# Moving the g_pre product of five first-norm tiles from the vector engine to GpSimd, and the rstd into the scale of the fp16 split

## The chip, the cores and the metric

The kernel runs on one core of a Trainium2 chip. The metric is the device time of one execution in microseconds; the time of a kernel is the median of its runs. A profiled execution leaves a trace, whose span runs from the first to the last instruction on the core; its own time is a little longer than that span. The engines are named as in the trace: PE is TensorE's matrix multiply and PEld its weight load, DVE is VectorE, ACT is ScalarE, POOL is GpSimd and SP is SyncE, which here only issues DMAs.

## What is computed

One layer of a hybrid decoder trunk on a sequence of 1024 tokens, 1024 wide, in float32. What matters here is its beginning, the first norm and the projection that follows it:

```python
def rms_norm(x, g):
    var = jnp.mean(x * x, axis=-1, keepdims=True)
    return x * lax.rsqrt(var + RMS_EPS) * g

h = rms_norm(x, norm_mix_pre)                 # x: 1024 tokens x 1024
proj = h @ w_in                               # q, k, v, conv inputs, two gates
q, k, v, cb, cc, cx, g_att, g_conv = split(proj)
m = sigmoid(g_att) * (attention(q, k, v) @ w_att) + sigmoid(g_conv) * (conv(cb, cc, cx) @ w_conv)
x = x + rms_norm(m @ w_out, norm_mix_post)
# then a convolutional feed-forward of width 2816, with a norm of its own
```

The attention is stick-breaking and strictly causal, in 8 heads of 64.

## The kernel before

**Precision.** Products of matrices are made of fp16 pairs. A float32 operand is scaled by a power of two and split into a high half (the fp16 rounding) and a low half (the rest), and three passes of fp16 matmuls, high by high, high by low and low by high, stand for one float32 product. The scale of the normed activations is `s_h`, a power of two worked out from the largest gain.

**Tiles.** The tokens are eight tiles of 128 (tile 0 to 7), each a [128 tokens, 1024] float32 tile `x`, loaded by SP at the start. A tile is normed and then turned, so that the model dimension lies on the partitions, into `hT` (high and low half). Tiles 0 to 2 are turned by PE. Tiles 3 to 7 are split first and then turned by the DMA's transpose, and these five are the ones that the change touches.

**One of these five tiles, before.** `norm` (line 253): ACT squares the row and sums it (`sumsq`, line 66); DVE makes mean plus epsilon (line 256, a 128x1 instruction); GpSimd raises it to the power of -0.5 (line 257, 128x1), which gives rstd; DVE multiplies the tile in place by rstd, a scalar for each partition, and by `gb`, the gain broadcast to all partitions (line 259, 128x1024). `turn_dma` (line 302): ACT writes the high half, the tile times `s_h` rounded to fp16 (line 304, 128x1024); DVE writes the low half, the tile times `s_h` less the high half (line 305, 128x1024); SP issues a DMA transpose for each half (line 308).

**What surrounds them.** PE makes the value products `pv` (line 367) of tiles 0 to 3, then the q and the k of the first head pair for the first 512 tokens (line 459, `pq` and `pk`), then the values of tile 4, then attention scores `z` (line 595) between further projections ("fills"). ACT and DVE split the weights on their way: `wh_v` at lines 520 and 522, `wh_q` and `wh_k` at lines 445 and 446. They also take the high and low half of q and k out of the accumulator (lines 474 and 476), move the value tiles (lines 381 to 398), and finish the turned tile 2 (lines 526 and 527) and tile 0 (lines 543 and 544).

**Order.** Inside this part nothing is ordered by hand on any engine but PE. Each step is put into a plan with its engine, an assumed cost, what it reads and what it writes; a list scheduler then runs through all of them with those costs and writes out one order for each engine: "V" for DVE, "A" for ACT, "G" for GpSimd, "SP" for the queue of SP, and "PE". Each engine works through its instructions in that order. Most PE steps keep the order in which they are written; the scores, the weighted values and the sums of the weight scales are fitted in where the plan has them ready. A step's rank among those that are ready comes from how late it may be for what follows it, or from a due time that it is given (tiles 4, 5, 6 and 7 have 0, 3, 4 and 5 us). The tile of rstd (`r_pre`) comes from a ring of 8 small tiles.

Of the kernel before, what the change touches and what calls it, by code (L numbers as in the profile page):

```python
# [20 lines left out]
AF = mybir.ActivationFunctionType  # L21
ALU = mybir.AluOpType
# [20 lines left out]
TURNED = (0, 1, 2, 4, 5, 6)  # L43
KEPT = (3,)
ONE = 2.0 ** 14


class Layer:
# [84 lines left out]
    def mixer(self, mid):  # L133
        tc, nc, a = self.tc, self.nc, self.a
        hT = self.hp.tile([P, 2, KD, T], F16, tag="hT", name="hT")
        with ExitStack() as ph1:
# [6 lines left out]
            nc.gpsimd.memset(self.mask[:, :NH], 0.0)  # L143
            nc.gpsimd.memset(self.mask[:, NH:], ONE)
            nc.gpsimd.affine_select(self.mask[:, NH:], self.mask[:, NH:], [[1, P]], ALU.is_ge, 0.0, base=0,
# [5 lines left out]
            if True:  # L151
# [7 lines left out]
                gb = self.slot([P, D], F32, "g_pre")  # L159
                xt = {}  # L160
# [25 lines left out]
                with tc.manual_schedule(engines={ET.PE, ET.DVE, ET.Activation, ET.SP, ET.Pool}):  # L186
                    pl = Plan(dict(s=12, ws=4, wh=8, pm=3, z=2, o=1, sm=8, rb=8, sc=16, e=3, w=2, wt=1, cr=4, o16=4))
                    pl.landed = 0.9
                    pl.own, pl.loaded = {"PE": 0.0}, 22.0
                    vec, act, pe, pool = nc.vector, nc.scalar, nc.tensor, nc.gpsimd  # L190
                    NOTE = lambda: Buf(None, lambda: {})

                    def given(p, tile, avail=0.0):
                        b = Buf(p, None)
                        b.tile, b.avail = tile, avail
                        pl.caps[p] -= 1
                        return b

                    def V(cost, fn, r, w, **kw):
                        return pl.add("V", cost, fn, r, w, **kw)  # L200

                    def A(cost, fn, r, w, **kw):
                        return pl.add("A", cost, fn, r, w, **kw)

                    def M(cost, fn, r, w, seq=True):
                        return pl.add("PE", cost, fn, r, w, seq=seq)

                    def two_banks(name):
                        return pat.tile([P, KD, P], F32, tag="z", name=name, bufs=2)
# [7 lines left out]
                    gbb = given("s", gb, 14.4)  # L217
# [6 lines left out]
                    g_s, g_c, g_t = NOTE(), NOTE(), NOTE()  # L224
                    h0, h1 = slice(0, NH), slice(NH, D)
                    s_h, inv_h = gs[:, 3:4], gs[:, 4:5]
# [19 lines left out]
                    gpb = Buf("z", lambda: two_banks("g_ps"))  # L246
                    ps2 = Buf("pm", lambda: pm.tile([P, NH], F32, tag="pm", name="g2"))
                    for c in range(2):
                        M(0.94, lambda c=c: pe.matmul(gpb.t.rearrange("p k t -> p (k t)")[:, ds(c * NH, NH)], on1[0:1, :],
                                                      gr[0:1, ds(c * NH, NH)], start=True, stop=True), [one_row, g_row], [(gpb, str(c))])  # L250
                    M(0.3, lambda: pe.matmul(ps2.t[:, 0:2], self.ones[0:1, :], g_c.t["g16"][0:1], start=True, stop=True),
                      [g_c], [ps2])
                    def norm(tt):
                        r, x = Buf("sm", lambda: self.small(f"r_pre{tt}")), xs[tt]
                        A(1.25, lambda: self.sumsq(xt[tt], r.t[:, 0:1], f"n_pre{tt}"), [x], [r])
                        V(0.15, lambda: vec.tensor_scalar(r.t[:, 1:2], r.t[:, 0:1], 1.0 / D, EPS, ALU.mult, ALU.add), [], [r])
                        pl.add("G", 0.6, lambda: pool.tensor_tensor(r.t[:, 2:3], r.t[:, 1:2], self.neghalf, ALU.pow), [], [r])
                        g = gpb if tt < 2 else gbb
                        V(1.28, lambda: vec.scalar_tensor_tensor(
                            xt[tt], xt[tt], r.t[:, 2:3], g.t.rearrange("p k t -> p (k t)") if tt < 2 else gb,  # L260
                            ALU.mult, ALU.mult), [r, g], [x])

                    def norm_halves(tt, first=(), prior=(), then=None):
                        r, x = Buf("sm", lambda: self.small(f"r_pre{tt}")), xs[tt]
# [36 lines left out]

                    def turn_dma(tt, due=1e9):
                        b, x = Buf("s", lambda: self.slot([P, 2, D], F16, f"x16_{tt}")), xs[tt]
                        A(1.06, lambda: act.activation(b.t[:, 0, :], xt[tt], AF.Copy, scale=s_h), [x, g_s], [(b, "0")], due=due)
                        V(1.27, lambda: vec.scalar_tensor_tensor(b.t[:, 1, :], xt[tt], s_h, b.t[:, 0, :], ALU.mult, ALU.subtract),
                          [x, g_s, (b, "0")], [(b, "1")], due=due)
                        for e in range(2):
                            j = pl.add("SP", 1.27, lambda e=e: nc.sync.dma_start_transpose(hT[:, e, :, ds(tt * P, P)], b.t[:, e, :]),
                                       [(b, str(e))], [(hb[tt], str(e))], due=due + 5)
                            j.load = 1.0  # L310
# [210 lines left out]
                    for i in range(4):  # L521
                        V(1.25, lambda i=i: vec.scalar_tensor_tensor(wvb[i].t[:, 1, :], st[i], bv.t["s"], wvb[i].t[:, 0, :],
                                                                     ALU.mult, ALU.subtract), [raw_v[i], bv, (wvb[i], "0")], [(wvb[i], "1")])
                    norm(2)
                    turn_pe(2)
                    A(1.1, lambda: act.activation(hT[:, 0, :, ds(2 * P, P)], pt[2].t, AF.Copy, scale=s_h), [pt[2], g_s], [(hb[2], "0")])
# [9 lines left out]
                    for i in range(4):  # L536
                        v_pass(1, (2 * i, 2 * i + 1), ((0, 1),), last=i == 3)
                    v_end(0)
                    norm(3)
                    turn_dma(3)  # L540
                    v_pass(2, range(8), ((0, 1),), last=True)
                    v_end(1)
# [12 lines left out]
                    for tt, due in ((4, 0.0), (5, 3.0), (6, 4.0), (7, 5.0)):  # L555
                        norm(tt)
                        turn_dma(tt, due)
# [39 lines left out]
                    def unit(u):  # L597
# [23 lines left out]
                        for h in range(2):  # L621
                            def scan(h=h):
                                x = e.t[:, h, NH - w:][:, ::-1]
                                vec.tensor_tensor_scan(x, x, m[:, ::-1], ONE if diag else cr.t[:, h:h + 1], ALU.mult, ALU.max)  # L624
                            V(0.08 + 1.13 * r, scan, [] if diag else [cr], [(e, str(h))], due=PACE[1])
# [8 lines left out]
                        def turn(x):  # L634
                            pl.add("SP", 1.25, lambda: nc.sync.dma_start_transpose(
                                wt.t[:, x, :2 * w // P, ds(t * P, P)], w16.t[:, x, :2 * w]),
                                [(w16, str(x))], [(wt, f"{x}{t}")], due=PACE[4]).load = 1.5 * r
                        A(0.21 + 0.85 * r, lambda: act.activation(dst(0), src(), AF.Copy, bias=-ONE), [e], [(w16, "0"), turns[2]], due=PACE[2])  # L638
                        turn(0)

                        def low():
                            if not diag:
                                f = lambda x: w16.t[:, x, :2 * w].rearrange("p (h s) -> p h s", h=2)
                                vec.scalar_tensor_tensor(f(1), e.t[:, :, NH - w:], ONE, f(0), ALU.subtract, ALU.subtract)
                                return
                            for h in range(2):
                                vec.scalar_tensor_tensor(dst(1)[:, h], src()[:, h], ONE, dst(0)[:, h], ALU.subtract, ALU.subtract)
                        V(0.08 + 1.1 * r + 0.08 * diag, low, [e, (w16, "0")], [(w16, "1")], due=PACE[3])
# [32 lines left out]
                    k = 0  # L681
# [1324 lines left out]
```

## Time and profile before

| | us |
|---|---|
| median of 3 runs | 1250.1 |
| lowest and highest of the runs | 1249.38, 1251.72 |
| profiled execution, its own time | 1250.39 |
| span of the profiled execution | 1248.7 |
| PE busy in the span | 1233.2 |

In the views, a row of the timeline gives the start of an instruction in us from the span's start, its duration, the engine, the line, the operation with what it writes and reads, and in brackets how long its engine was idle before it and what ended that. A row of the windows gives a stretch and the busy time of each engine in it, with the number of instructions, then the clock granted to TensorE as a share of full speed, the busy share of the DMA engines and GB/s. A row of waits gives who waited for whom, the total in us, how often, and the longest.

### The profile page before, as it was taken

To read this page: it belongs to the slowest core of one execution; us is meant where nothing else is said; L and a number is where in the kernel's file an instruction comes from. 1 tells how busy PE (TensorE), PEld (TensorE's weight loads), DVE (VectorE), ACT (ScalarE), POOL (GpSimd) and SP (SyncE) were. 2 spreads that over 40 slices of the span, in tenths; PEclk is the share of its full clock that TensorE was granted. 3 is DMA by queue.
4 is the path that set the end of the run, shared out by engine and by line. 5 is a ranking of instruction groups with operands and counts; after the bars stand their busy time and mean duration, and the time that the engine had idled before them with its cause. 6 is when DMAs were issued, how large, how long until landed. Compare 5 with 4: busy or idle time off the path is not lost.

```text
span 1248.7 us, 16478 instructions
## 1 busy us (share of the span) xinstructions
PE 1233.2 (99%) x6065; PEld 559.4 (45%) x6065; DVE 1018.6 (82%) x1605; ACT 856.1 (69%) x1247; POOL 86.3 (7%) x113
## 2 busy tenths in 40 slices
PE   9999999999999999999989999999999999999997
PEld 4444444444444444444444444444444444444443
DVE  7888889856998675559899999699589879969866
ACT  7766666736758565755666679778778967878434
POOL 1100000000000000001100001001100300111003
PEclk9999999999999999999999999999999999999999
DMA  8755577660224111656953205415921961594607
GB/s 276 157 128 116 136 129 180 148 150 29 74 74 129 34 65 54 233 189 149 222 144 133 71 23 214 169 34 99 257 82 19 203 184 34 104 251 142 179 1 135
DMA packets 148931, 160.80 MB, mean 129 GB/s; under 512 B 114425, under 2 KB 114553, under 8 KB 148850
## 3 DMA queue, kind: packets, MB, share of 16 engines
q1 hardware_dynamic: 138480, 123.05, 35.3%
q0 software_dynamic: 10368, 36.70, 14.1%
q8 instruction: 47, 0.77, 0.3%
q14 instruction: 34, 0.28, 0.1%
q10 hardware_dynamic: 2, 0.00, 0.0%
HBM read 92.88 MB, written 37.75 MB: 105 GB/s over the span
## 4 chain that ended last, share of the span: by engine, by line
PE 45%; DVE 2%; DMA 2%; issue 1%; ACT 1%; POOL 1%; POOLq 0%; DVEq 0%; SPq 0%; ACTq 0%
PE pq L1601 12%; PE pd L1671 2%; PE pu6b L1425 1%; PE pu10b L1425 1%; PE pu8b L1425 1%; PE pu20b L1425 1%; PE pu19b L1425 1%; PE pu16b L1425 1%; PE pu12b L1425 1%; PE pu4b L1425 1%; PE pu3b L1425 1%; PE pu21b L1425 1%; PE pu18b L1425 1%; PE pu17b L1425 1%; PE pu15b L1425 1%
## 5 line engine op out<-in xcount | busy, mean ns | idle before, releaser
L1425 PEld LDWEIGHTS <-wh_u 128*128 128x128 f16 x1848 | 179.1, 98 | 219.0 <-issue 2.2
L824 ACT ACTIVATE wh_u<-ws_u,sc_u 128x1024 f16<-128x1024 f32 (+1 forms) x66 | 66.5, 1010 | 36.8 <-PE pr_dn L812 7.4
L993 PEld LDWEIGHTS <-wh_g 128*128 128x128 f16 x588 | 57.0, 98 | 68.6
L1605 ACT ACTIVATE st<-pq,sd 128x512 f32<-128x512 f32 x112 | 75.3, 696 | 11.8 <-PE pq L1601 8.6
L1228 PE MATMUL py<-wo,m 128*128 128x512 f16 x384 | 83.3, 379 | 0.0
L826 DVE SCALAR_TENSOR_TENSOR wh_u<-ws_u,sc_u,wh_u 128x1024 f16<-128x1024 f32 (+1 forms) x66 | 72.5, 1104 | 10.4 <-ACT wh_u L824 10.2
L790 POOL DMA_DIRECT2D acc<-st x56 | 43.8, 783 | 426.6 <-ACT st L1605 426.6
L624 DVE TENSOR_TENSOR_SCAN e<-e,mask 128x512 f32<-128x512 f32 (+3 forms) x64 | 48.7, 807 | 13.2 <-ACT e L617 13.2
L1228 PEld LDWEIGHTS <-m 128*128 128x128 f16 x384 | 37.4, 98 | 44.9
L1474 DVE SCALAR_TENSOR_TENSOR ug<-cg,cw_g,ug 128x1023 f32<-128x1023 f32 (+1 forms) x44 | 56.2, 1278 | 1.3 <-ACT ug L1472 1.3
L1474 DVE SCALAR_TENSOR_TENSOR ua<-ca,cw_a,ua 128x1023 f32<-128x1023 f32 (+1 forms) x44 | 56.2, 1278 | 1.1 <-ACT ua L1472 0.9
L617 ACT ACTIVATE e<-z,cz 128x1024 f32<-128x1024 f32 (+3 forms) x48 | 42.3, 896 | 20.4 <-PE z L595 14.8
L66 ACT ACTIVATE jk_u<-ws_u 128x1024 bf16<-128x1024 f32 x44 | 46.5, 1056 | 12.4 <-DMA ws_u<-w_up_nt 12.2
L638 ACT ACTIVATE w<-e 128x1024 f16<-128x1024 f32 (+3 forms) x48 | 38.8, 837 | 12.4 <-DMA wt<-w 6.3
L459 PE MATMUL pcc<-hT,wh_cc 128*128 128x512 f16 x192 | 44.6, 380 | 0.8 <-ACT u L575 0.8
L459 PE MATMUL pk<-hT,wh_k 128*128 128x512 f16 x192 | 43.1, 379 | 0.0
L459 PE MATMUL pq<-hT,wh_q 128*128 128x512 f16 x192 | 43.0, 379 | 0.0
L1601 PE MATMUL pq<-wq,fx 128*128 128x512 f16 x192 | 42.8, 379 | 0.0
L1601 PE MATMUL pq<-wq,fy 128*128 128x512 f16 x192 | 42.7, 379 | 0.0
L923 PE MATMUL pywc<-p,wh_wc 128*128 128x512 f16 x192 | 42.6, 379 | 0.0
L1601 PE MATMUL pq<-wq,fs 128*128 128x512 f16 x192 | 42.2, 379 | 0.0
L624 DVE TENSOR_TENSOR_SCAN e<-e,cr,mask 128x512 f32<-128x512 f32 x32 | 39.8, 1273 | 1.2 <-ACT e L617 1.0
(796 smaller groups left out, 2731.1 us busy)
## 6 DMA issues: line engine op xcount, KB each, us to landing
acc<-st POOLq DMA_DIRECT2D x56, 512.0 KB, 5.9
ws_u<-w_up_nt SPq DMA_DIRECT2D x44, 512.0 KB, 4.1
ds<-w_down SPq DMA_DIRECT2D x18, 512.0 KB, 14.8
wt_g<-w_in_nt SPq DMA_DIRECT2D x14, 512.0 KB, 3.5
x<-x SPq DMA_DIRECT2D x8, 512.0 KB, 8.6
wr_wo<-w_out SPq DMA_DIRECT2D x8, 512.0 KB, 3.6
ws_wo<-w_out SPq DMA_DIRECT2D x8, 512.0 KB, 4.3
xr<-x SPq DMA_DIRECT2D x8, 512.0 KB, 4.3
```

What stands on the lines that cost most here:

```text
L66: self.nc.scalar.activation(self.junk(f"jk_{name}"), src, AF.Square, accum_out=acc)
L459: pe.matmul(ps.t, w.t[:, wi, ds(k * P, P)], hT[:, hi, k, ds(c * NH, NH)], start=k == 0 and p == 0, stop=k == KD - 1 and p == 2)
L624: vec.tensor_tensor_scan(x, x, m[:, ::-1], ONE if diag else cr.t[:, h:h + 1], ALU.mult, ALU.max)
L790: j = pl.add(eng, 0.45 if eng == "SP" else 1.14, lambda: e.dma_start(dst(), srcf(), **kw), r, [b] if w is None else w, ahead=AHEAD["load"] ...
L824: A(C["As" if big else "Ash"], lambda: act.activation(dst.t[:, 0, dsl], src.t[:, ssl], AF.Copy, scale=sb.t["s"]), [(src, sreg), sb], [(dst ...
L826: V(C["V" if big else "Vh"], lambda: vec.scalar_tensor_tensor(dst.t[:, 1, dsl], src.t[:, ssl], sb.t["s"], dst.t[:, 0, dsl], ALU.mult, ALU. ...
L993: pe.matmul(b.t, p.w[wt].t[:, wi, ds(wc * NH + k * P, P)], block(i, h, k), start=first and n == 0, stop=n == 3 * KH - 1, skip_group_check= ...
L1228: pe.matmul(b.t, m16[k].t[:, h_, ds(tt * P, P)], wo[k].t[:, w_, sl], start=k == 0 and p == 0, stop=k == 7 and p == 2)
L1425: pe.matmul(b.t, p.w[wt].t[:, wi, ds(wc * NH + k * P, P)], block(i, h, k), start=first and n == 0, stop=n == 3 * KH - 1, skip_group_check= ...
L1474: V(C["V"], lambda lag=lag: vec.scalar_tensor_tensor(u.t[:, lag:], c.t[:, :T - lag], sm.t[:, 2 - lag:3 - lag], u.t[:, lag:], ALU.mult, ALU ...
L1601: pe.matmul(b.t, fa[p].t[:, h, ds(fo * NH + tt * P, P)], wa[p].t[:, x, ds(wo * NH, NH)], start=first and n == 0, stop=n == 5, skip_group_c ...
L1605: A(C["Ah"], lambda tt=tt, b=b, st=st: act.activation(st.t[:, tt % 2, :], b.t, AF.Copy, scale=q.sd.t[:, 0:1]), [b, q.sd], [(st, str(tt % 2 ...
```

## The change

For tiles 3 to 7, DVE's product by rstd and gain is taken away. GpSimd multiplies the tile in place by the broadcast gain alone, once ACT has read the tile for its sum of squares. DVE makes one 128x1 product, rstd times `s_h`, and this takes the place of `s_h` as the scale of the high half on ACT and of the low half on DVE. Both halves now wait for GpSimd's product and for that 128x1 product, and the small tile of rstd is kept until the low half is written. In the plan the new GpSimd step has a cost of 2.4 us, against 1.28 us for the DVE step that is gone. For tile 2 the code keeps its DVE product.

```diff
+GAINED = (3,4,5,6,7,)
...
+                    rs = {}
+
                     def norm(tt):
                         r, x = Buf("sm", lambda: self.small(f"r_pre{tt}")), xs[tt]
+                        rs[tt] = r
                         A(1.25, lambda: self.sumsq(xt[tt], r.t[:, 0:1], f"n_pre{tt}"), [x], [r])
                         V(0.15, lambda: vec.tensor_scalar(r.t[:, 1:2], r.t[:, 0:1], 1.0 / D, EPS, ALU.mult, ALU.add), [], [r])
                         pl.add("G", 0.6, lambda: pool.tensor_tensor(r.t[:, 2:3], r.t[:, 1:2], self.neghalf, ALU.pow), [], [r])
-                        g = gpb if tt < 2 else gbb
-                        V(1.28, lambda: vec.scalar_tensor_tensor(
-                            xt[tt], xt[tt], r.t[:, 2:3], g.t.rearrange("p k t -> p (k t)") if tt < 2 else gb,
-                            ALU.mult, ALU.mult), [r, g], [x])
+                        if tt in GAINED:
+                            V(0.12, lambda: self.mul(r.t[:, 3:4], r.t[:, 2:3], s_h), [g_s], [r])
+                            pl.add("G", 2.4, lambda: pool.tensor_tensor(xt[tt], xt[tt], gb, ALU.mult), [gbb], [x])
+                        else:
+                            V(1.28, lambda: vec.scalar_tensor_tensor(xt[tt], xt[tt], r.t[:, 2:3], gb, ALU.mult, ALU.mult), [r, gbb], [x])
...
                     def turn_dma(tt, due=1e9):
                         b, x = Buf("s", lambda: self.slot([P, 2, D], F16, f"x16_{tt}")), xs[tt]
-                        A(1.06, lambda: act.activation(b.t[:, 0, :], xt[tt], AF.Copy, scale=s_h), [x, g_s], [(b, "0")], due=due)
-                        V(1.27, lambda: vec.scalar_tensor_tensor(b.t[:, 1, :], xt[tt], s_h, b.t[:, 0, :], ALU.mult, ALU.subtract),
-                          [x, g_s, (b, "0")], [(b, "1")], due=due)
+                        sc, dep = ((lambda: rs[tt].t[:, 3:4]), rs[tt]) if tt in GAINED else ((lambda: s_h), g_s)
+                        A(1.06, lambda: act.activation(b.t[:, 0, :], xt[tt], AF.Copy, scale=sc()), [x, dep], [(b, "0")], due=due)
+                        V(1.27, lambda: vec.scalar_tensor_tensor(b.t[:, 1, :], xt[tt], sc(), b.t[:, 0, :], ALU.mult, ALU.subtract),
+                          [x, dep, (b, "0")], [(b, "1")], due=due)
```

## Rows read from the trace of the kernel before

**Rows 1.** The page, part 1: busy time, share and instructions by engine.
```profile
PE 1233.2 (99%) x6065; PEld 559.4 (45%) x6065; DVE 1018.6 (82%) x1605; ACT 856.1 (69%) x1247; POOL 86.3 (7%) x113
```

**Rows 2.** Windows: stretch, length, then each engine's busy time (count), clock, DMA.
```profile
22.00:27.00 5.00, 4.74 (x24) 2.00 (x22) 4.56 (x6) 4.64 (x6) 1.52 (x1) 1.00 0.76 245
...
27.00:32.00 5.00, 5.00 (x27) 2.29 (x26) 4.29 (x11) 4.81 (x10) 0.86 (x2) 1.00 0.92 122
...
37.00:42.00 5.00, 5.00 (x25) 2.29 (x24) 5.00 (x7) 3.78 (x6) 2.79 (x2) 1.00 0.66 157
...
42.00:48.00 6.00, 6.00 (x30) 2.69 (x29) 6.00 (x10) 3.65 (x6) 0.00 (x0) 1.00 0.89 205
...
100.00:200.00 100.00, 98.09 (x619) 43.45 (x618) 85.10 (x158) 66.48 (x98) 0.00 (x0) 1.00 0.66 133
...
200.00:400.00 200.00, 199.31 (x1042) 90.00 (x1040) 164.76 (x256) 134.17 (x195) 0.00 (x0) 1.00 0.43 109
```

**Rows 3.** Waits of the weight loads, 20 to 52 us: total, times, longest.
```profile
PEld L367 <- DVE hT L527: 0.8, 1, 0.8
...
PEld L367 <- DMA hT<-x: 0.3, 1, 0.3
```

**Rows 4.** Timeline of PE: start, duration, line, operation, count [idle before].
```profile
26.74 3.19 PE L367 MATMUL pv<-wh_v,hT 128*128 128x512 f16 x14 [0.26 <-DVE hT L527]
...
47.52 4.05 PE L367 MATMUL pv<-wh_v,hT 128*128 128x512 f16 x18
...
51.50 1.31 PE L595 MATMUL z<-k,q 64*128 64x512 f16 x12
```

**Rows 5.** Groups of DVE, 27 to 51 us: busy us, mean ns | idle before.
```profile
L259 DVE SCALAR_TENSOR_TENSOR x<-x,r_pre,g_pre 128x1024 f32<-128x1024 f32 x4 | 5.0, 1281 | 0.0
...
L78 DVE TENSOR_TENSOR cz<-cz,cst 128x1 f32<-128x1 f32 x1 | 0.2, 159 | 0.0
```

**Rows 6.** Timeline of GpSimd: constants at the start, then the roots of the norm.
```profile
0.95 0.53 POOL L143 MEMSET mask<- 128x512 f16 x1
...
1.42 0.20 POOL L144 MEMSET mask<- 128x128 f16 x1
...
1.67 0.29 POOL masks.py:199 TENSOR_SCALAR_AFFINE_SELECT ident<-ident 128x128 f32<-128x128 f32 x1
...
22.65 1.52 POOL L257 TENSOR_TENSOR r_pre<-r_pre,neghalf 128x1 f32<-128x1 f32 x1 [6.15 <-DVE r_pre L256]
...
30.79 0.55 POOL L257 TENSOR_TENSOR r_pre<-r_pre,neghalf 128x1 f32<-128x1 f32 x1 [6.62 <-DVE r_pre L256]
...
37.19 1.53 POOL L257 TENSOR_TENSOR r_pre<-r_pre,neghalf 128x1 f32<-128x1 f32 x1 [4.03 <-DVE r_pre L256]
```

**Rows 7.** Timeline of DVE: around tile 3, then two later splits.
```profile
22.49 1.27 DVE L522 SCALAR_TENSOR_TENSOR wh_v<-ws_v,s0v,wh_v 128x1024 f16<-128x1024 f32 x1
...
24.21 1.28 DVE L259 SCALAR_TENSOR_TENSOR x<-x,r_pre,g_pre 128x1024 f32<-128x1024 f32 x1 [0.44 <-POOL r_pre L257]
...
25.41 1.28 DVE L527 SCALAR_TENSOR_TENSOR hT<-pt_pre,g_pre,hT 128x1024 f16<-128x1024 f32 x1
...
27.80 1.28 DVE L305 SCALAR_TENSOR_TENSOR x<-x,g_pre,x 128x1024 f16<-128x1024 f32 x1
...
37.03 1.29 DVE L446 SCALAR_TENSOR_TENSOR wh_k<-ws_k,sc_k,wh_k 128x1024 f16<-128x1024 f32 x1
...
49.91 0.69 DVE L476 SCALAR_TENSOR_TENSOR k<-pk,k 128x512 f16<-128x512 f32 x1
```

**Rows 8.** Timeline of ACT: tile 3's squares and copy, the first k copy.
```profile
21.42 0.18 ACT L66 ACTIVATION_READ_ACCUMULATOR jk_n_pre<-x 128x1 f32 x1
...
25.53 1.15 ACT L304 ACTIVATE x<-x,g_pre 128x1024 f16<-128x1024 f32 x1 [0.36 <-DVE x L259]
...
47.78 0.60 ACT L474 ACTIVATE k<-pk 128x512 f16<-128x512 f32 x1 [0.19 <-PE pk L459]
```

**Rows 9.** Line 308, the transposes: their time from issue to landing.
```profile
DMA to landing us min/median/max: 3.1/3.3/4.5
```

## The prediction, made before the changed kernel was run

> **What bounds the kernel now.** I read the page's busy shares first: PE is busy 99% of the span [rows 1], so only what makes PE wait, or spares it a wait, can move the time. Then the windows around the tiles that change. The five first norms fall between 20 and 50 us. There PE is busy in every microsecond from 27 on, while DVE is busy 4.29 of 5 us from 27 to 32 and all of the time from 37 to 48 [rows 2]: DVE is full beside a PE that is full. The granted clock is 1.00, which is the 2.4 GHz level, so no time hides there. PE's waits show what a lighter DVE could give back: 0.26 us at 26.74 for the low half of turned tile 2 [rows 4] (the weight load counts 0.8 for the same wait) and 0.3 us for the transposes of tile 3 [rows 3]. That is 0.5 us in all. From 100 to 200 us PE is idle 1.91 us, from 200 to 400 us 0.69 [rows 2]; no more is to be had in the rest of this plan. The gain is thus capped near 3 us, and only 0.5 us of it stands where the change works; a loss has no such cap, since a PE that is full cannot make up a wait.
>
> **What is removed.** Five DVE products of 1.28 us (line 259; four of them in 27 to 51 us sum to 5.0) [rows 5]. Back to back, DVE starts an instruction a little before the one ahead ends (line 259 at 24.21 lasts 1.28, line 527 behind it starts at 25.41, 1.20 later) [rows 7], so each is worth 1.2 us of DVE's queue, 6.0 in all.
>
> **What is added on DVE.** Five products of 128x1, priced by the row of such a product, 0.16 us [rows 5]: 0.8 us. The wait that they bring is for the root on GpSimd, which DVE already waited for (0.44 us ahead of tile 3's product) [rows 7].
>
> **What is added on GpSimd.** Five products of 128x1024 with two float32 inputs. The trace has no such instruction. Bounds: a fill of 512 fp16 columns took 0.53 us, of 128 columns 0.20, so 0.86 ns a column with no input read; 1024 columns would be 0.20 + 896 x 0.00086 = 0.97 us. A select with one input took 0.29 us for 128 float32 columns [rows 6]; eight of these are 2.3 us. The product reads two inputs, so it is nearest to the upper row: I take 2.3, and keep 1.0 for the range. 2.3 us five times is no load for GpSimd, which is all but idle here. The question is what DVE does meanwhile.
>
> **GpSimd and DVE side by side.** The root on one column takes 0.55 us when DVE is idle (30.79). When it is issued into a long DVE instruction with two operands in the on-chip memory it takes 1.5 (22.65, 37.19) [rows 6], and it ends 0.4 us behind that instruction: 22.65 + 1.52 = 24.17 against 22.49 + 1.27 = 23.76, and 37.19 + 1.53 = 38.72 against 37.03 + 1.29 = 38.32 [rows 7]. So GpSimd does not go slower beside DVE, it stands still until DVE's instruction is over. The trace never shows the reverse, DVE standing still for GpSimd, because GpSimd never had anything long. Bounds: nothing, if DVE always goes first, or the full 2.3 us for each product. I take the full hold: two engines that exclude each other as sharply as these rows show will do so whoever began, and a product that waits gets in between two DVE instructions, as the root did.
>
> The Trainium skill (SBUF — State Buffer, "Who interferes with whom") says that a DVE instruction with two SBUF inputs and a GpSimd instruction that reads SBUF exclude each other, and that whoever began keeps the second one out to its end. The trace agrees for the one direction that it shows (0.55 to 1.5 us); by the rule the sum below is +2.3 us, by a reading in which only GpSimd ever waits it is -0.5. The price that the skill gives (GPSIMD Engine Reference, "Performance versus the Vector engine": 4497 ns for an add of 2048 columns) would, halved, make the sum 0.1 us smaller.
>
> **The sum, place by place.** What counts is PE's lateness at each place that it waits at.
>
> *Tile 2's low half, 26.74.* Tile 3's squares are read out by 21.60 [rows 8], so the product can be had then, before the root, which needs a DVE instruction first; by the plan's greedy rule the product most likely goes first on GpSimd and the root queues behind it. It gets in where the third `wh_v` split would start, 22.50, and holds that split until 24.8. Before, the split started at 22.49 and line 527 at 25.41, with tile 3's product and its 0.44 us of waiting between [rows 7]. After, the split starts at 24.8 and line 527 at 24.8 + 1.2 = 26.0, 0.6 late. PE's wait grows from 0.26 to about 0.85 us: +0.6.
>
> *Tile 3's transposes, 32.3.* The root behind the product meets the held split (24.8 to 26.07) and ends 0.4 behind it, 26.5; DVE is then in line 527 to 27.3, the 128x1 product follows, to 27.45; ACT's high half runs 27.55 to 28.7 (before, from 25.53 [rows 8], with ACT's queue standing behind it for the difference); the low half 28.7 to 30.0, where it ran 27.80 to 29.08 [rows 7]. That is 0.9 late, and the transposes land some 3.3 us after issue [rows 9] as before. PE, already 0.6 late, waits 0.3 more: +0.9 together.
>
> *The first scores, 51.50.* They need the low half of k, written at 49.91 to 50.60 [rows 7], so 0.9 us is in hand. DVE's queue up to there: four products gone, -4.8; four of 128x1, +0.6; four holds of 2.3, +9.2; net +5.0 us. Some of it finds cover: DVE's idle time from 27 to 32, 0.7 us [rows 2]; the low half of q, which takes only one operand from the on-chip memory, 0.7 like that of k [rows 7]; and eight or so of the fifteen short 128x1 instructions that the code has here (four at line 256, the others in the scales of q and k), at 0.16 each [rows 5], 1.3. That is 2.7. With the 0.9 us from tile 3 the low half of k is 0.9 + 5.0 - 2.7 = 3.2 us late, less the 0.9 in hand: PE is 2.3 us late at its first scores. The three places lie on one path, so 2.3 is the total and not a term to be added to 0.9. Behind it, DVE is 85% busy and catches up, but PE stays full [rows 2] and keeps its lateness.
>
> SP's queue issues the same ten transposes in this stretch, in the plan's order; one that waits for a late half holds the value moves (line 385) behind it, which the 18 value matmuls from 47.52 [rows 4] give time for. No load is added. The small tile of rstd lives longer, five of a ring of eight at most, and the next user of the ring is a weight's sum far behind.
>
> So 1250.39 + 2.3 = 1252.7 against the profiled execution's own time, which lies 0.3 above the median of the runs; against the median, 1252.4. A measurement of this kernel tells about 0.2%, 2.5 us, from no change, so the forecast is a small loss just inside that.
>
> **Rivals.**
>
> *A. DVE is not held.* GpSimd waits in its gaps, DVE takes no notice, or the product is short (1.0 us, when four holds of 4.0 replace 4.8). For it: DVE's rows next to the root show no stretching. Against: the sharp exclusion of the root. DVE is then 6.0 - 0.8 = 5.2 us lighter, but PE has only its two waits to give back: -0.5, 1249.6, or as before if tile 3's chain through GpSimd uses that up.
>
> *B. The plan pulls the scores forward (slower).* The plan charges DVE nothing for GpSimd's work and believes it 5 us lighter, so it can have k's low half directly behind ACT's high half, which ends at 47.78 + 0.60 = 48.38 [rows 8], not at 49.91: scores 1.5 us earlier in PE's order, with fewer of the 18 value matmuls ahead of them [rows 4]. On the chip the low half is as late as before and PE has 1.5 us less to do: 2.3 + 1.5 = +3.8, 1253.9; without the 2.7 us of cover, 6.5. For it: the order comes from those costs alone. Against: the value matmuls keep their written order, and the scores are fitted between. It decides as soon as fewer than about 11 value matmuls (18 less 1.5 / 0.22 us) stand ahead of the first scores.
>
> *C. A real gain.* The lighter DVE moves the whole plan forward and the 1.91 us of PE's waits from 100 to 200 us go with the 0.5: -2.4, 1247.7. Against: these waits lie 50 us behind the change, where DVE is not full.
>
> **How the numbers follow.** Forecast, +1 to +5 us: 0.50, of which I put 0.32 below +2.5 and 0.18 above. A: 0.23. B: 0.22, nearly all above +2.5. C: 0.05. Within 0.2%: 0.32 + 0.23 = 0.55. Slower: 0.18 + 0.22 = 0.40. Faster: 0.05. The range reaches from A (1249.6, with a little of C, 1249.4) to the forecast without any cover, 0.9 + 5.0 - 0.9 = +5.0, and the larger part of B: 1256.0. The likeliest case alone is 1251.1 to 1255.1.
>
> **What the profile would show.** Right: GpSimd products over 2 us each in 20 to 45 us, some longer for waiting; two-operand DVE instructions (lines 522, 544, 446, 305) that run beside them and last 2 to 3.5 us in place of 1.28, or start late after idle time put down to GpSimd; PE waits before 27, near 32 and at the first scores that sum to about 2.8 us, 2.3 more than now. Wrong: DVE's instructions keep 1.28 us next to GpSimd's products and DVE has gaps in 37 to 48 us (A); the first scores stand well before 50 us in PE's order with a wait for line 476 (B); PE idle from 100 to 200 us much under 1.9 (C). A root ahead of the product on GpSimd would take away the lateness at tile 3 but not at the scores. What would make it wrong altogether is a new order on ACT or SP that holds a weight split behind a waiting high half.

## The result, and the profile after

The changed kernel took 1253.46 us (median of 9 runs, 1252.29 to 1254.34) beside 1250.1 for the kernel before (median of 9). The ratio is 1.0023, with a 95% interval of 1.0013 to 1.0033, so the change costs 2.9 us (1.6 to 4.1); the medians themselves lie 3.4 us apart. The forecast was 1252.4, +2.3. The loss is small, near the 0.2% (2.5 us) that the prediction took as the least that a measurement tells from no change, but no change lies outside its interval. The profiled execution took 1253.86 us, 3.5 more than that of before. Line numbers are 1 to 7 higher in the changed kernel: the low half of tile 2 is line 533 (was 527), the split of `wh_v` 528 (522), the scores 601 (595).

First the busy shares on the page of the changed kernel:

```profile
PE 1232.7 (98%) x6065; PEld 558.5 (45%) x6065; DVE 1022.8 (82%) x1605; ACT 855.6 (68%) x1247; POOL 96.1 (8%) x118
```

Then its windows, which answer to [rows 2]:

```profile
27.00:32.00 5.00, 4.64 (x23) 2.14 (x24) 3.35 (x10) 4.91 (x10) 2.66 (x2) 1.00 0.90 142
...
37.00:42.00 5.00, 5.00 (x25) 2.27 (x24) 5.00 (x5) 3.39 (x6) 3.17 (x2) 1.00 0.30 61
...
100.00:200.00 100.00, 99.92 (x630) 44.25 (x629) 84.52 (x158) 64.79 (x97) 0.00 (x0) 1.00 0.63 131
...
200.00:400.00 200.00, 198.62 (x1036) 89.27 (x1035) 164.68 (x251) 134.08 (x194) 0.00 (x0) 1.00 0.43 109
```

PE does the same work (1232.7 us against 1233.2), so the loss is waiting. DVE lost 6 us of work to GpSimd and still counts 1022.8 us busy, 4.2 more than before: its instructions have become longer. From 37 to 42 us it is as full as before with 5 instructions in place of 7. And from 100 to 200 us PE, idle for 1.91 us before [rows 2], is idle for 0.08.

Next the timeline of GpSimd in the changed kernel; a bracket is the idle time ahead and what ended it:

```profile
19.83 2.74 POOL L264 TENSOR_TENSOR x<-x,g_pre 128x1024 f32<-128x1024 f32 x1 [3.38 <-ACT jk_n_pre L67]
22.53 1.52 POOL L261 TENSOR_TENSOR r_pre<-r_pre,neghalf 128x1 f32<-128x1 f32 x1
29.34 2.50 POOL L264 TENSOR_TENSOR x<-x,g_pre 128x1024 f32<-128x1024 f32 x1 [5.29 <-ACT jk_n_pre L67]
...
32.33 2.35 POOL L264 TENSOR_TENSOR x<-x,g_pre 128x1024 f32<-128x1024 f32 x1
...
38.83 5.74 POOL L264 TENSOR_TENSOR x<-x,g_pre 128x1024 f32<-128x1024 f32 x2 [3.65 <-ACT jk_n_pre L67]
```

And DVE beside them:

```profile
20.33 4.51 DVE L528 SCALAR_TENSOR_TENSOR wh_v<-ws_v,s0v,wh_v 128x1024 f16<-128x1024 f32 x2
24.77 0.15 DVE L79 TENSOR_TENSOR r_pre<-r_pre,g_pre 128x1 f32<-128x1 f32 x1
24.84 1.27 DVE L528 SCALAR_TENSOR_TENSOR wh_v<-ws_v,s0v,wh_v 128x1024 f16<-128x1024 f32 x1
26.03 1.27 DVE L533 SCALAR_TENSOR_TENSOR hT<-pt_pre,g_pre,hT 128x1024 f16<-128x1024 f32 x1
...
30.63 0.16 DVE L72 TENSOR_SCALAR sc_q<-pr_q 128x1 int32<-128x1 int32 x1 [0.87 <-PE pr_q L349]
...
32.39 2.31 DVE L79 TENSOR_TENSOR r_pre<-r_pre,g_pre 128x1 f32<-128x1 f32 x1 [0.57 <-POOL r_pre L261]
...
38.99 3.38 DVE L311 SCALAR_TENSOR_TENSOR x<-x,r_pre,x 128x1024 f16<-128x1024 f32 x1
...
42.36 2.24 DVE L79 TENSOR_TENSOR r_pre<-r_pre,g_pre 128x1 f32<-128x1 f32 x1
```

The product that met least resistance took 2.35 us (32.33). Beside four of the five, a DVE instruction with two operands in the on-chip memory lasts 2.0 to 2.2 us longer than alone: two splits of `wh_v` 4.51 us (alone 1.28 and 1.20 behind each other, so 2.0 too much), the low half of line 311 3.38 for 1.28, and twice a product of one column, 2.31 and 2.24 for 0.15. Together 8.4 us. The fifth product, tile 4's at 29.34, met only the tail of a DVE instruction, waited it out, and then had DVE idle or on short instructions of one operand, which keep their length beside it (30.63, 0.16).

PE's timeline, the rows with a wait from 18 to 100 us (there are no others over 0.1 us):

```profile
27.36 3.19 PE L373 MATMUL pv<-wh_v,hT 128*128 128x512 f16 x14 [1.84 <-DVE hT L533]
...
51.27 0.39 PE L601 MATMUL z<-k,q 64*128 64x512 f16 x2 [0.37 <-ACT k L480]
53.46 1.10 PE L601 MATMUL z<-k,q 64*128 64x512 f16 x10 [1.79 <-DVE k L482]
...
59.62 5.12 PE L465 MATMUL pq<-hT,wh_q 128*128 128x512 f16 x23 [1.21 <-DMA hT<-x]
```

The release at tile 2's place comes at 27.36 against 26.74 [rows 4], 0.62 later on the clock of the trace. But the two executions do not start alike. PE reaches the 20 matmuls ahead of this place 0.96 us earlier than in the profile of before (21.04 against 22.00), and DVE is earlier by as much: its first split of `wh_v`, here in the kernel before and then in the changed one, starts at 20.03 and 19.07.

```profile
20.03 1.28 DVE L522 SCALAR_TENSOR_TENSOR wh_v<-ws_v,s0v,wh_v 128x1024 f16<-128x1024 f32 x1
...
19.07 1.28 DVE L528 SCALAR_TENSOR_TENSOR wh_v<-ws_v,s0v,wh_v 128x1024 f16<-128x1024 f32 x1
```

Executions of the same order differ by as much: in the kernels below that share the changed kernel's order on PE up to there, the scale matmul `pr_v` ahead of the first split starts anywhere from 15.57 to 16.50 us (15.76 here, 16.72 before). What makes the start differ is not shown, and neither is whether the new order starts earlier on the average; the clock column of the windows reads 1.00 there in both executions. So the start is taken out here, and what counts is by how much a wait has grown. From the first split to the low half of tile 2 DVE takes 5.38 us before (20.03 to 25.41 [rows 7]) and 6.96 now (19.07 to 26.03), and PE's wait has grown by the same 1.58 us (1.84 - 0.26). From there the waits add, 0.37 + 1.79 + 1.21 = 3.37, so PE is 4.95 us late. From 100 to 200 us it wins back 1.91 - 0.08 = 1.83, and from 200 to 400 it loses 1.38 - 0.69 = 0.69. Sum by the waits: +3.81, inside the measured 1.6 to 4.1. Between the two profiled executions the early start takes 0.96 of it away, which leaves 2.85 of their 3.5 us; the other 0.6 us was not traced.

The waits that are gone stood here in the kernel before (PE's timeline, the rows with a wait in 100 to 200 us):

```profile
113.54 0.39 PE L595 MATMUL z<-k,q 64*128 64x512 f16 x2 [0.74 <-ACT k L474]
114.31 0.61 PE L595 MATMUL z<-k,q 64*128 64x512 f16 x4 [0.38 <-DVE k L476]
166.37 1.46 PE L459 MATMUL pcc<-hT,wh_cc 128*128 128x512 f16 x6 [0.78 <-ACT u L575]
```

### The profile page after: what moved, and what is told of

It is laid out like the page before. It is cut to its first block, busy times and chain, and to the rows that moved or that the text cites. A ratio compares the mean times of both kernels' runs of the same rounds, so it can differ in the third digit from the quotient of the medians.

```text
span 1252.2 us, 16472 instructions
## 1 busy us (share of the span) xinstructions
PE 1232.7 (98%) x6065; PEld 558.5 (45%) x6065; DVE 1022.8 (82%) x1605; ACT 855.6 (68%) x1247; POOL 96.1 (8%) x118
## 4 chain that ended last, share of the span: by engine, by line
PE 45%; DVE 2%; DMA 1%; ACT 1%; issue 1%; POOL 1%; POOLq 0%; DVEq 0%; ACTq 0%
PE pq L1607 12%; PE pd L1677 2%; PE pu10b L1431 1%; PE pu6b L1431 1%; PE pu20b L1431 1%; PE pu19b L1431 1%; PE pu16b L1431 1%; PE pu12b L1431 1%; PE pu8b L1431 1%; PE pu4b L1431 1%; PE pu3b L1431 1%; PE pu21b L1431 1%; PE pu18b L1431 1%; PE pu17b L1431 1%; PE pu15b L1431 1%
```

## The experiments

All ratios are against the kernel before, run on the same chip. The plan's order is the difficulty: it is made from the costs that are written beside each step, so an edit that changes a cost also changes the order of all that follows. The first four kernels separate the two: the order of before or the new one, with GpSimd's products or without their weight.

**The order of before, with GpSimd's products.** The planned costs are those of before, so that PE, DVE, ACT and SP have the order of before; the product is put in at no cost.

```diff
-V(0.12, lambda: self.mul(r.t[:, 3:4], r.t[:, 2:3], s_h), [g_s], [r])
-pl.add("G", 2.4, lambda: pool.tensor_tensor(xt[tt], xt[tt], gb, ALU.mult), [gbb], [x])
+pl.add("G", 0.0, lambda: pool.tensor_tensor(xt[tt], xt[tt], gb, ALU.mult), [], [x])
+V(1.28, lambda: self.mul(r.t[:, 3:4], r.t[:, 2:3], s_h), [r, gbb, g_s], [x, r])
```

> The GpSimd products as in the change, but every engine's order as in the kernel before: in the plan the 128x1 product stands in the place of the old DVE product and at its cost of 1.28 us, and the GpSimd product costs nothing. Theory H (GpSimd's product holds DVE's two-operand instructions, and that alone costs the time): the holds are there, so +2 to +4 us over before, 1252 to 1254, with PE waits for tile 2's low half (1.5 to 2 us) and for the first scores behind all 18 value matmuls (1 to 2 us). Theory O (the plan, which takes DVE for lighter than it is, writes a worse order): the old order is back, so 1249.6 to 1250.6. Theory L (GpSimd's product and root make tile 3's own chain longer, DVE is not held): a wait at tile 3's transposes alone, +0.5 to +1.

Measured: 1256.26 us, ratio 1.0049 (1.0037 to 1.0061), +6.1 us, worse than the change with its own order and than the 2 to 4 us expected. PE's timeline at tile 2's place and around the first scores:

```profile
27.25 3.19 PE L373 MATMUL pv<-wh_v,hT 128*128 128x512 f16 x14 [1.17 <-DVE hT L533]
...
53.36 0.39 PE L601 MATMUL z<-k,q 64*128 64x512 f16 x2 [0.40 <-ACT k L480]
55.88 1.43 PE L601 MATMUL z<-k,q 64*128 64x512 f16 x10 [2.12 <-DVE k L482]
57.23 2.74 PE L373 MATMUL pv<-wh_v,hT 128*128 128x512 f16 x6
```

DVE's timeline in the same kernel, two rows next to products, and the low halves of tile 3 and of k:

```profile
22.08 3.31 DVE L528 SCALAR_TENSOR_TENSOR wh_v<-ws_v,s0v,wh_v 128x1024 f16<-128x1024 f32 x1
...
28.30 1.28 DVE L311 SCALAR_TENSOR_TENSOR x<-x,r_pre,x 128x1024 f16<-128x1024 f32 x1
...
29.56 3.36 DVE L550 TENSOR_TENSOR hT<-h,hT 128x1024 f16<-128x1024 f32 x1
...
55.14 0.68 DVE L482 SCALAR_TENSOR_TENSOR k<-pk,k 128x512 f16<-128x512 f32 x1
```

And one of its windows, behind the first scores:

```profile
57.00:58.00 1.00, 1.00 (x4) 0.28 (x3) 0.33 (x1) 1.00 (x2) 0.00 (x0) 0.50 0.82 142
```

DVE stands still here too (3.31 and 3.36 us for 1.28 and 1.21), and beside the other three products too (2.29 and 2.33 for 0.15, and two instructions in a row 2.92 for 0.75). PE's wait at tile 2's place is 1.17 us, 0.91 more than before; then PE waits 0.73 at the small matmul for k's scale, 0.40 and 2.12: 4.16 us late at the first scores. Behind the wait of 2.12 us the granted clock is 0.50, the 1.2 GHz level: six matmuls of 128x512 take 2.74 us where six take 1.47 at the full clock, and the ten scores ahead of them 1.43 for 1.10. That is 1.6 us more. The sum, 5.8, is near the 6.1 measured. The three waits at 113 and 166 us are there as before.

**The new order, with the product cut to one column.**

```diff
-pool.tensor_tensor(xt[tt], xt[tt], gb, ALU.mult)
+pool.tensor_tensor(xt[tt][:, 0:1], xt[tt][:, 0:1], gb[:, 0:1], ALU.mult)
```

> The changed kernel with its orders unchanged on every engine, but GpSimd multiplies one column of each tile in place of 1024 (the gain of tiles 3 to 7 is thus left out but for that column). DVE is as light as the change makes it and is not held. Theory H: all the loss goes; the two short waits of before go too; 1249.0 to 1250.0, 0.3 to 1 us under before. Theory O: the order alone costs, so 1252.5 to 1253.5 as after the change.

Measured: 1247.85 us, ratio 0.9986 (0.9977 to 0.9994), -1.8 us, more than the 0.3 to 1 us expected. PE has one wait left between 20 and 220 us (the view of waits: total, times, longest):

```profile
PE o L601 <- DMA wt<-w: 0.4, 1, 0.4
```

**The order of before, with the product cut to one column.** The edit of the first experiment, with the product on column 0 alone.

> The fourth corner: the order of before and GpSimd's product on one column only (gain of tiles 3 to 7 left out but for that column). DVE is lighter than before by 5 x 1.2 less 5 x 0.15 us and not held. Theory H: what a lighter DVE is worth without any price, 0.3 to 0.6 us under before (PE's waits of 0.26 and 0.28 go). Theory O: the same. The difference from the one-column kernel with the new order is what the order alone does: H says under 0.7 us, O says 2.5 or more.

Measured: 1249.71 us, ratio 0.9997 (0.9989 to 1.0006). DVE has room now (2.05 of 5 us busy from 37 to 42, where it was full), the 0.26 us wait for tile 2 is gone, and the time is that of before. The waits from 100 to 200 us did not move:

```profile
PE pcc L465 <- ACT u L581: 0.8, 1, 0.8
PE z L601 <- ACT k L480: 0.7, 1, 0.7
PE z L601 <- DVE k L482: 0.4, 1, 0.4
```

So a lighter DVE by itself is worth nothing that can be measured, and the gain of the one-column kernel in the new order belongs to the order: 1.4 us between the two ratios, between what the theories expected (under 0.7, or 2.5 and more).

**Is it GpSimd's reading that holds DVE?** The new order; GpSimd fills the tile twice, which takes it nearly as long (1.96 us against 2.35) and reads nothing.

```diff
-pl.add("G", 2.4, lambda: pool.tensor_tensor(xt[tt], xt[tt], gb, ALU.mult), [gbb], [x])
+pl.add("G", 2.4, lambda: [pool.memset(xt[tt], 1.0) for _ in range(2)], [gbb], [x])
```

> The changed kernel, orders unchanged, with GpSimd filling each tile twice with ones in place of the product (so tiles 3 to 7 carry ones times rstd): GpSimd is busy about 2 x 1.0 us a tile from the fills at the start, but reads nothing. Theory H with the hold in what GpSimd reads: DVE's instructions keep 1.28 us beside the fills and the time is near the one-column kernel, 1249 to 1250.5. Theory H with any GpSimd work holding DVE: holds of 2 us, 1252 to 1253.5.

Measured: 1249.28 us, ratio 0.9998 (0.9989 to 1.0006). The timelines of GpSimd and DVE at tile 3:

```profile
20.40 1.96 POOL L264 MEMSET x<- 128x1024 f32 x2 [3.91 <-ACT jk_n_pre L67]
22.33 1.62 POOL L261 TENSOR_TENSOR r_pre<-r_pre,neghalf 128x1 f32<-128x1 f32 x1
...
21.07 2.47 DVE L528 SCALAR_TENSOR_TENSOR wh_v<-ws_v,s0v,wh_v 128x1024 f16<-128x1024 f32 x2
```

With the fills beside them, two splits take 2.47 us, as when alone. The root, which reads, is still held (1.62 for 0.55). GpSimd's time is thus not the matter; that it reads is. The Trainium skill (SBUF — State Buffer, "Who interferes with whom") says just this: a DVE instruction with two SBUF inputs contends with a GpSimd instruction that reads SBUF, not with one that only writes it. The trace agrees on both sides, 2.0 us of hold for the product and none for the fill.

**The product by the gain on DVE,** early, with rstd still folded into the split: no load on GpSimd, no load off DVE.

```diff
-pl.add("G", 2.4, lambda: pool.tensor_tensor(xt[tt], xt[tt], gb, ALU.mult), [gbb], [x])
+V(1.28, lambda: vec.tensor_tensor(xt[tt], xt[tt], gb, ALU.mult), [gbb], [x])
```

> As the change, rstd folded into the scale, but the product with the gain is on DVE (a product of two tensors, 1.28 us in the plan) as soon as the squares are read. DVE carries what it carried before plus the 128x1 products, GpSimd only the roots. Theory H: no hold, so none of the 5.6 us; 1249 to 1251 by where the plan's new order falls. If folding rstd (the later scale, one more dependence) costs by itself, 1251.5 or more.

Measured: 1251.67 us against 1250.42, ratio 1.0009 (1.0001 to 1.0018), +1.1. That is above the 1251.5 that the expectation named for a cost of the folding itself. But the kernel makes an order of its own, with waits of 0.4 to 1.0 us at five other places, so it does not tell a cost of the folding from a cost of the order.

**The new order with the old work.** GpSimd's step is planned and issues nothing; DVE makes the product of before, by rstd and gain, where the change has its 128x1 product, and the scale of the halves is `s_h` again. The plan sees the change, the engines do the work of before.

```diff
-V(0.12, lambda: self.mul(r.t[:, 3:4], r.t[:, 2:3], s_h), [g_s], [r])
-pl.add("G", 2.4, lambda: pool.tensor_tensor(xt[tt], xt[tt], gb, ALU.mult), [gbb], [x])
+V(0.12, lambda: vec.scalar_tensor_tensor(xt[tt], xt[tt], r.t[:, 2:3], gb, ALU.mult, ALU.mult), [g_s], [r])
+pl.add("G", 2.4, lambda: None, [gbb], [x])
...
-sc, dep = ((lambda: rs[tt].t[:, 3:4]), rs[tt]) if tt in GAINED else ((lambda: s_h), g_s)
+sc, dep = ((lambda: s_h), rs[tt]) if tt in GAINED else ((lambda: s_h), g_s)
```

> Every engine's order as in the changed kernel, but the work of the kernel before: DVE's product by rstd and gain at the place of the 128x1 product, nothing on GpSimd but the roots, the scale again the common one. If the new order is worth 1.8 us by itself (one-column kernels: 1247.85 against 1249.71) and DVE's 5.2 us of extra work finds room in that order: 1247.8 to 1248.8, faster than before. If the order only fits a lighter DVE, the low halves of q and k come late: 1250.5 to 1253.

Measured: 1249.31 us against 1250.42, ratio 0.9991 (0.9982 to 0.9999), -1.1 us (-2.2 to -0.1), between the two ranges expected. This is the fastest version that computes the reference, ahead of both kernels, if by little. Its timeline of PE at tile 2's place:

```profile
26.39 3.20 PE L373 MATMUL pv<-wh_v,hT 128*128 128x512 f16 x14 [0.93 <-DVE hT L533]
```

And all its PE waits from 20 to 220 us:

```profile
PE pv L373 <- DVE hT L533: 0.9, 1, 0.9
PE o L601 <- DMA wt<-w: 0.3, 1, 0.3
```

Against before: a wait 0.93 - 0.26 = 0.67 longer at tile 2, 1.91 - 0.35 = 1.56 less idle time from 100 to 200 us, 0.69 more from 200 to 400: -0.2 by the waits, at the edge of what was measured. Against the change, which has the same order: 1.84 - 0.93 = 0.91 at tile 2, then 3.37 of waits, less 0.27 (its wait for `wt`), 4.0 in all; the ratios differ by 0.0032, 4.0 us.

**Tiles 4 to 7 alone, and tile 3 alone.** `GAINED = (4, 5, 6, 7)` and `GAINED = (3,)`.

> The change for tiles 4 to 7 only; tile 3 keeps its DVE product. Theory H by place: the wait of 1.8 us for tile 2's low half goes, the waits at the first scores and at the tiles' transposes stay: 1251 to 1252.5. If the loss sits at the first scores whatever comes before, as the forecast took it: 1253 or more.

> The change for tile 3 only. Theory H by place: one hold in front of tile 2's low half, 1.5 us of PE wait and nothing later: 1251 to 1252. If a single early hold is caught up by the first scores: 1249.5 to 1250.5.

Measured: 1255.95 us, ratio 1.0048 (1.0036 to 1.0060), and 1256.6, ratio 1.0053 (1.0041 to 1.0065), against 1250.42. Each part costs twice the whole, and both lie above the ranges of the expectations that went by place. PE's timeline with tiles 4 to 7, and a window behind its last wait:

```profile
25.80 3.19 PE L373 MATMUL pv<-wh_v,hT 128*128 128x512 f16 x14 [0.26 <-DVE hT L533]
52.95 0.39 PE L601 MATMUL z<-k,q 64*128 64x512 f16 x2 [1.44 <-ACT k L480]
54.94 1.57 PE L601 MATMUL z<-k,q 64*128 64x512 f16 x10 [1.60 <-DVE rb_q L344]
```

```profile
56.00:58.00 2.00, 2.00 (x8) 0.59 (x5) 1.26 (x2) 1.50 (x2) 0.00 (x0) 0.50 1.03 190
```

The same two views with tile 3 alone:

```profile
28.25 3.19 PE L373 MATMUL pv<-wh_v,hT 128*128 128x512 f16 x14 [1.85 <-DVE hT L533]
...
187.23 1.47 PE L601 MATMUL z<-k,q 64*128 64x512 f16 x6 [2.69 <-ACT e L623]
```

```profile
187.00:189.00 2.00, 1.77 (x8) 0.49 (x9) 2.00 (x5) 1.40 (x3) 0.00 (x0) 0.50 0.40 114
```

Without tile 3's product PE's wait at tile 2's place is 0.26 us, as before, so that place is tile 3's doing. (It is released at 25.80, 0.94 earlier than before: an early start again.) The other four then put the loss at the scores, where two waits close together end in a low clock. With tile 3 alone the order is yet another: PE's wait at tile 2's place is 1.85 us, as in the change, a wait of 1.0 us for transposes follows, and one of 2.69 us appears at 187 us, some 150 us behind the change, again with the low clock behind it. Both kernels keep the three waits at 100 to 200 us; neither has the new order's gain.

**The root ahead of the product.** The product is made to wait for the root (`[gbb, r]` in place of `[gbb]`).

> The changed kernel, but on GpSimd each tile's root stands ahead of its product (the product waits for it); PE and SP keep their order. Theory H (the holds): the same five products hold DVE as long, so 1252.5 to 1254.5. Theory L (the queue of product and root on GpSimd makes the tile's chain long): the scale is there 2 us earlier, PE's wait for tile 2's low half shrinks from 1.8 to under 1, and 1 to 1.5 us come back: 1251.5 to 1252.3.

Measured: 1254.93 us against 1251.04, ratio 1.0036 (1.0023 to 1.0048), no better than the change. The root does come first, and yet the timelines of GpSimd, DVE and PE show:

```profile
20.60 2.35 POOL L264 TENSOR_TENSOR x<-x,g_pre 128x1024 f32<-128x1024 f32 x1
...
20.66 2.31 DVE L79 TENSOR_TENSOR r_pre<-r_pre,g_pre 128x1 f32<-128x1 f32 x1 [0.44 <-POOL r_pre L261]
...
27.81 4.65 PE L373 MATMUL pv<-wh_v,hT 128*128 128x512 f16 x14 [2.48 <-DVE hT L533]
```

GpSimd goes straight from the root to the product, 0.06 us ahead of DVE's 128x1 product, which reads two operands and stands for 2.31 us. The remedy undoes itself; PE waits 2.48 us, and the 14 matmuls behind the wait take 4.65 us where the change's take 3.19: from 28 to 31 us the granted clock is 0.53.

**Tile 2's low half moved ahead** (`due=-6.0` on line 533), once with the old work in the new order, once in the changed kernel.

> The kernel before's work in the new order (as the run before, 1249.31), and the low half of turned tile 2 gets a due time in the plan, which puts it ahead of tile 3's product and of the third and fourth split of the value weights on DVE. PE's one remaining wait of 0.9 us in 20 to 100 us should go: 1248.2 to 1248.8, under before by 1.5 to 2 us. If the late value weight split then makes PE wait instead: 1249 to 1250.

> The changed kernel, GpSimd's products as they are, with the due time for the low half of turned tile 2 alone: on DVE it moves ahead of the third and fourth split of the value weights; SP and GpSimd keep their orders. Theory H by place, and by operands: that instruction reads only one operand from the on-chip memory (the other lies in the accumulator), so it is not held by tile 3's product; PE's wait of 1.8 us at this place goes, the waits at the first scores and the second-half transposes stay: 1.2 to 1.8 us back, 1251.5 to 1252.3. Rival: the hold only moves to the splits behind it and PE waits for those instead, or the 1.8 us are lost again at the first scores: 1253 to 1254.

Measured: 1249.95 us, ratio 0.9994 (0.9985 to 1.0003), no different from the same kernel without the edit by this measurement, and not the 1.5 to 2 us under before that were expected; and 1254.95 against 1250.75, ratio 1.0037 (1.0023 to 1.0050). The changed kernel gains nothing from losing the wait at tile 2: the expectation's rival was right, not its 1.2 to 1.8 us back. PE's rows in it:

```profile
29.63 0.16 PE L349 MATMUL pr_q<-rb_q,ones 128*128 128x1 bf16 x1 [1.10 <-DVE r_pre L260]
51.15 0.39 PE L601 MATMUL z<-k,q 64*128 64x512 f16 x2 [0.83 <-ACT k L480]
53.34 1.10 PE L601 MATMUL z<-k,q 64*128 64x512 f16 x10 [1.80 <-DVE k L482]
```

The scores stand at 53.34, against 53.46 in the change, with starts 0.13 us apart. DVE releases them in both, so the wait that is saved at tile 2 comes back further on, as 1.10 us at 29.63 and 0.83 for 0.37 at 51.15. The waits lie on one path, as the prediction had it.

## Why the prediction was right

**DVE held by GpSimd: right, in full.** The trace of before showed only GpSimd held by DVE. That it goes the other way too, for the whole instruction, shows in 2.0 to 2.2 us on four of five products in the change and on all five in the order of before, and the fill that reads nothing holds nothing. The product's own price, taken as 2.3 with 1.0 for the range, is 2.35. (One sum beside it is off: at half of 4497 ns each of the four holds would be 0.05 us shorter, 0.2 in all and not 0.1.)

**Tile 2: the place and the hold right, the size too small.** Forecast 0.6, the low half starting at 26.0. The trace of the change shows 0.62 and 26.03, but by luck, since that execution starts 0.96 early; PE's wait grows by 1.58. The new order makes 0.67 of it (the wait of the kernel with the old work) and the hold 0.91. In the order of before, which the working assumed, it is 0.91 too: there the 128x1 product, with 0.44 us of waiting for the root, stands ahead of the low half and not behind it.

**Tile 3: no wait of its own.** Forecast 0.3 more; PE has no wait between 28 and 50 us. Tile 3's low half starts at 27.23 (line 311, was 27.80), or 0.4 us late with the start taken out, where the forecast had 28.7 and 0.9.

**First scores: the path right, the loss too small.** Forecast 2.3 us late in all; measured 1.58 + 0.37 + 1.79 = 3.74, and 4.16 in the order of before, which the working assumed. The term that was mis-sized is the cover, "that is 2.7". From tile 3's low half to k's low half DVE takes 22.11 us before (27.80 to 49.91 [rows 7]) and 26.84 in the first experiment (28.30 to 55.14), 4.73 more, where the sum had 5.0 - 2.7 = 2.3: the cover was about 0.3. DVE's idle time between the two even grew, from 0.84 to 1.47 us. The short products of 128x1 were entered as 0.16 us each and as cover; two of the change's own, which read two operands, were held for 2.3 and 2.2 us instead. Only tile 4's product found DVE free.

**Not in the sum: transposes of later tiles, 1.21 us.** At 59.62 PE waits for them; the kernel with the same order and the old work has no such wait, so GpSimd's products make it. The prediction had given SP's queue no cost.

**Rivals.** A, no hold, is excluded by the rows of DVE. B, the plan pulling the scores forward, happened in part: 12 value matmuls (48.14, 2.75 us) in place of 18 stand directly ahead of the first scores, where the prediction had set the mark at fewer than about 11. Its price did not follow: the wait there is 2.16 us, against 2.52 in the order of before. C, the gain from 100 to 200 us, had a chance of 0.05 and came: 1.83 us. It came by the plan's new order and not by a lighter DVE on the chip: a lighter DVE with the order of before leaves these waits untouched (ratio 0.9997); the new order with the old work removes them (0.9991).

Put together by ratios, where the order and the holds are crossed:

| | DVE not held by products | GpSimd's products in full |
|---|---|---|
| order of before | 0.9997 (one column) | 1.0049 |
| new order | 0.9986 (one column), 0.9991 (old work) | 1.0023 |

In the new order the products cost 4.0 us over the old work (0.0032). Of that, some 3.1 us is the hold itself, by the kernel that fills instead (1.0023 - 0.9998). The remainder is the root's longer queue less what a lighter DVE gives, about 1 us, which is the size of these intervals. The order gave 1.1 us back by the ratios (0.1 to 2.2), 0.2 by the waits. So +2.3 came near +2.9 in part by luck, through two errors of opposite sign: the products cost more than forecast (4.0), and the order, which the forecast took as unchanged, gave something back. The mechanism, a DVE that is held and a PE that cannot make up a wait, was right.

**Open.** Why tile 3 alone makes an order with a wait of 2.69 us at a place 150 us later was not traced to a step of the plan. Whether the holds can be steered into DVE's idle time, as tile 4's was by chance, was not tried.

## What to carry to other kernels

Before work goes from DVE to GpSimd, price it by what DVE does meanwhile: here a product of 2.35 us, which reads the on-chip memory, made the DVE instruction with two operands there that it met 2.0 to 2.2 us longer, to take 1.2 us from DVE. Where a list of costs makes the order, the order is a term of its own, of -1 to several us here, and a kernel that has the new plan with the old work, beside one with the old plan and the new work, tells it from the change. Before two traces are laid side by side, take out the difference of their starts: here it moved PE and DVE alike by 0.96 us, so that the end of a wait moved by 0.62 while the change had cost 1.58.

## What the hardware showed that was not expected

A DVE product of one column, 0.15 us alone, lasted 2.31 us beside GpSimd's product: the hold goes by what an instruction reads and not by its size. A GpSimd instruction that waits gets in between two DVE instructions that stand back to back (20.33, where two splits became 4.51 us). And PE's granted clock stayed at 1.00 behind waits of 1.85, 1.84 and 1.79 us, and behind 0.83 and 1.80 close together, but was 0.50 in stretches behind waits of 2.12, 2.48 and 2.69 us, and behind 1.44 and 1.60 close together. Four of the five kernels with medians above 1254 us show this; in the first experiment it added 1.6 us to the wait.
